# Five homes for x, earlier transposes, and output stores on GpSimd's queue at the end of block 1 of a fused MLP kernel

## The chip, the cores and the metric

The kernel runs on one core of one Trainium2 chip. Times are microseconds (us) on the device, of one execution each; most executions of a kernel agree within 0.3%. A profile shows the span of one execution, from its first to its last instruction. PE is TensorE, DVE is VectorE, ACT is ScalarE, POOL is GpSimd, SP is SyncE; a trailing q (ACTq, SPq) is an engine's queue as it issues a transfer.

## The reference

```
y   = x @ w1 + b1            # x: 16 x 512 x 768, w1: 768 x 3072
y   = 0.5*y*(1 + erf(y/sqrt(2)))
out = y @ w2                 # w2: 3072 x 768, float32 out
```

## The kernel before

The rows are worked in eight blocks of 1024. A block's first product and gelu are units of one kind (`Unit1`), its second product units of others. Both products save multiplications by a Strassen-like scheme: sums of operands on VectorE, seven products instead of eight on TensorE. Block 1 ends in four "lean" units (`Unit2` with `lean`) that finish its second product and store the output, while SP writes prepared weight pieces to memory for later blocks (`w2s`), loads w1 for block 2 (`w1s`), and transposes x of block 2. All SBUF space is cut from one tile, so every home is a range that something else held before.

The parts that the change and the argument touch, with cuts marked:

```python
osbs1 = [[cut(XT_N + k * PAR, 2 * N2).bitcast(FP32),            # right half of an output row tile
          cut(XT_N + k * PAR + 2 * N2, 2 * N).bitcast(FP32)]    # full output row
         for k in range(2)]
spare = stage + [wb_at(2 * XT_N + o) for o in
                 (PAR, PAR + WB, XT_N, XT_N + WB, XT_N + 2 * WB)]
# ...
def xh_of(sb, t):                        # where x of block sb, tile t is loaded
    if sb < ONE:
        return cut(sb * GR + GR // 2 + t * K, K)
    return xh_late[t % 3]                # three homes
# ...
class Unit2:
    def __init__(self, g, sb, u):
        self.lean = sb > 0
        self.eng = nc.scalar if self.lean and u < 2 * NU - 1 else nc.sync   # stores' queue
        self.o = (osbs1 if self.lean else osbs)[u % 2]
    def right_done(self):
        self.eng.dma_start(out=orr[...], in_=self.o[0])         # L471
    def left_done(self, row, bank):
        # ...
        self.eng.dma_start(out=orr[...], in_=self.o[1])         # L482
# ...
def copy_xy(u):                          # seeds PSUM bank bY before products 7, 6, 4
    if isinstance(u, Unit2) and u.lean:
        nc.scalar.copy(out=bY[...], in_=u.rows(par1))           # L618
        return
    nc.scalar.copy(out=bY[...], in_=bX[...])                    # L620
```

## Time and profile before

| | first profiled execution | timed executions |
|---|---|---|
| time | 854.49 us | 851.46, 851.83, 851.99 us |
| span | 852.7 us | |
| PE busy, PE idle | 844.6, 8.1 us | |
| PE waits behind ScalarE, 222 to 236 us | 1.19 + 0.38 + 0.81 us | |

The prediction below shows the lines behind this table. The transfer side of the same stretch, by windows of time (busy us of PE, PEld, DVE, ACT and POOL, then clock, share of the 16 transfer engines, GB/s), before:

```profile
212.00:218.00 6.00, 6.00 (x38) 3.61 (x37) 5.31 (x8) 0.46 (x1) 0.00 (x0) 1.00 1.00 263
218.00:224.00 6.00, 4.82 (x31) 2.83 (x29) 2.69 (x5) 0.89 (x2) 0.53 (x1) 1.00 0.98 141
```

### The profile page before, as it was taken

To read this page: it belongs to the slowest core of one execution; us is meant where nothing else is said; L and a number is where in the kernel's file an instruction comes from. 1 tells how busy PE (TensorE), PEld (TensorE's weight loads), DVE (VectorE), ACT (ScalarE), POOL (GpSimd) and SP (SyncE) were. 2 spreads that over 40 slices of the span, in tenths; PEclk is the share of its full clock that TensorE was granted. 3 is DMA by queue.
4 is the path that set the end of the run, shared out by engine and by line. 5 is a ranking of instruction groups with operands and counts; after the bars stand their busy time and mean duration, and the time that the engine had idled before them with its cause. 6 is when DMAs were issued, how large, how long until landed. Compare 5 with 4: busy or idle time off the path is not lost.

```text
span 852.7 us, 16579 instructions
## 1 busy us (share of the span) xinstructions
PE 844.6 (99%) x6468; PEld 571.2 (67%) x6468; DVE 671.4 (79%) x1132; ACT 422.8 (50%) x692; POOL 85.9 (10%) x139
## 2 busy tenths in 40 slices
PE   9999999999999999999999999999999999999998
PEld 5444445696544798448974499645995469944798
DVE  5766679777756998579976799667996689956998
ACT  4777762221178512784138732577216771267611
POOL 5121100012000002100020000200012100010000
PEclk9999999999999999999999999999999999999999
DMA  9998787579999599996999689995999949985397
GB/s 229 197 282 172 165 187 276 211 217 215 249 353 226 175 318 379 293 203 228 330 367 314 128 279 336 359 276 133 312 346 343 299 106 318 351 323 171 100 306 287
DMA packets 144642, 220.82 MB, mean 259 GB/s; under 512 B 61916, under 2 KB 85396, under 8 KB 144564
## 3 DMA queue, kind: packets, MB, share of 16 engines
q1 hardware_dynamic: 117536, 178.36, 66.7%
q0 software_dynamic: 25696, 38.94, 21.0%
q10 hardware_dynamic: 1332, 2.47, 1.0%
q8 instruction: 50, 0.82, 0.4%
q14 instruction: 28, 0.23, 0.1%
HBM read 182.07 MB, written 47.87 MB: 270 GB/s over the span
## 4 chain that ended last, share of the span: by engine, by line
PE 92%; DMA 6%; DVE 1%; issue 0%; ACT 0%; POOL 0%; ACTq 0%; DVEq 0%
PE bY L409 21%; PE bY L514 15%; PE bX L409 14%; PE bX L514 10%; PE bZ L409 7%; PE bW L409 7%; PE bW L514 5%; PE bZ L514 5%; PE bY L454 3%; DMA arena<-in_x_dram 3%; DMA w2s<-arena 1%; PE bY L601 1%; DMA arena<-in_w_dram 1%; PE bW L454 1%; PE bX L601 1%; PE bZ L454 1%
## 5 line engine op out<-in xcount | busy, mean ns | idle before, releaser
L206 DVE TENSOR_TENSOR arena<-arena 128x1536 f16<-128x1536 f16 (+6 forms) x634 | 406.5, 672 | 7.8 <-DMA arena<-arena 1.3
L409 PEld LDWEIGHTS <-arena 128*128 128x128 f16 x1974 | 192.3, 98 | 226.0 <-issue 2.2
L514 PEld LDWEIGHTS <-arena 128*128 128x128 f16 x3528 | 292.1, 98 | 8.2
L409 PE MATMUL bY<-arena 128*128 128x512 f16 x846 | 214.5, 379 | 1.4 <-ACT bY L620 1.2
L627 DVE TENSOR_TENSOR arena<-bY,arena 128x512 f32<-128x512 f32 (+1 forms) x102 | 69.4, 680 | 121.9 <-PE bY L409 91.9
L620 ACT COPY bY<-bX 128x512 f32<-128x512 f32 (+1 forms) x144 | 79.1, 549 | 123.2 <-DVE arena L563 87.6
L514 PE MATMUL bY<-arena 128*128 128x192 f16 x1500 | 138.3, 246 | 0.0
L409 PE MATMUL bX<-arena 128*128 128x512 f16 x564 | 138.2, 379 | 0.0
L425 ACT ACTIVATE arena<-arena,b1t 128x1024 f16<-128x1024 f32 x94 | 108.0, 1149 | 52.9 <-DVE arena L655 52.9
L640 ACT COPY arena<-bW 128x512 f32<-128x512 f32 (+1 forms) x148 | 81.4, 550 | 89.1 <-PE bW L514 43.9
L514 PE MATMUL bX<-arena 128*128 128x192 f16 x1020 | 93.2, 246 | 0.0
L655 DVE TENSOR_TENSOR arena<-bZ,arena 128x512 f32<-128x512 f32 (+1 forms) x102 | 69.3, 679 | 20.2 <-PE bZ L409 18.2
L409 PE MATMUL bW<-arena 128*128 128x512 f16 x282 | 76.2, 379 | 0.0
L409 PE MATMUL bZ<-arena 128*128 128x512 f16 x282 | 76.2, 379 | 0.0
L546 POOL DMA_DIRECT2D out_dram<-arena x42 | 30.5, 728 | 409.1 <-DVE arena L651 331.8
L430 ACT ACTIVATE arena<-bX,b1t 128x512 f16<-128x512 f32 x94 | 64.0, 680 | 11.1 <-PE bX L409 7.9
L454 PEld LDWEIGHTS <-arena 128*128 128x128 f16 x480 | 46.8, 98 | 32.4 <-issue 1.6
L671 ACT COPY bZ<-bY 128x512 f32<-128x512 f32 (+1 forms) x58 | 30.8, 532 | 70.8 <-DVE arena L655 27.5
L430 ACT ACTIVATE arena<-bY,b1t 128x512 f16<-128x512 f32 x94 | 63.3, 673 | 0.0
L314 POOL DMA_DIRECT2D arena<-in_x_dram x60 | 32.6, 549 | 183.2 <-DMA arena<-arena 172.5
L514 PE MATMUL bZ<-arena 128*128 128x192 f16 x504 | 48.5, 246 | 0.0
L514 PE MATMUL bW<-arena 128*128 128x192 f16 x504 | 48.5, 246 | 0.0
(60 smaller groups left out, 411.1 us busy)
## 6 DMA issues: line engine op xcount, KB each, us to landing
arena<-w2s SPq DMA_DIRECT2D x300, 288.0 KB, 4.6
arena<-w1s SPq DMA_DIRECT2D x72, 672.0 KB, 7.4
out_dram<-arena POOLq DMA_DIRECT2D x42, 384.0 KB, 7.4
w2s<-arena SPq DMA_DIRECT2D x49, 288.0 KB, 4.2
arena<-in_x_dram POOLq DMA_DIRECT2D x60, 192.0 KB, 7.4
w1s<-arena SPq DMA_DIRECT2D x12, 672.0 KB, 6.1
arena<-in_w_dram POOLq DMA_DIRECT2D x17, 384.0 KB, 9.2
out_dram<-arena SPq DMA_DIRECT2D x9, 384.0 KB, 2.5
```

The lines of the kernel that those rows point to most:

```text
L206: nc.vector.tensor_tensor(out=o, in0=a, in1=b, op=op)
L314: nc.gpsimd.dma_start(out=xhs[t], in_=xr[:, sb * 8 + t, :])
L409: nc.tensor.matmul(out=dst[:, 0:RH], lhsT=w1_op(self.wt, slot)[:, c, :], rhs=a[:, c, :], start=first and c == 0, stop=c == self.C - 1, ski ...
L425: nc.scalar.activation(out=self.G[1][:, hi, :, :], in_=self.tmp, func=GELU, bias=b1t[:, 2 * hi + 1:2 * hi + 2])
L430: nc.scalar.activation(out=self.G[0][:, hi, row, :], in_=bank[:, 0:RH], func=GELU, bias=b1t[:, 2 * hi:2 * hi + 1])
L454: nc.tensor.matmul(out=dst[:, 0:N2], lhsT=a, rhs=w[:, :, c, :], start=first and c == 0, stop=c == self.C - 1, skip_group_check=True)
L514: nc.tensor.matmul(out=dst[:, t * N4:(t + 1) * N4], lhsT=a, rhs=w[:, c, :], start=first and c == 0 and t == ts[0], stop=c == NQ - 1, skip_ ...
L620: nc.scalar.copy(out=bY[u.g % 2][:, 0:u.F], in_=bX[u.g % 2][:, 0:u.F])
L627: nc.vector.tensor_tensor(out=u.c22(), in0=bY[u.g % 2][:, 0:u.F], in1=w[:, 0:u.F], op=ADD)
L640: nc.scalar.copy(out=w[:, 0:u.F], in_=bW[:, 0:u.F])
L655: nc.vector.tensor_tensor(out=u.c12(), in0=bZ[:, 0:u.F], in1=w[:, 0:u.F], op=ADD)
L671: nc.scalar.copy(out=bZ[:, 0:u.F], in_=bY[u.g % 2][:, 0:u.F])
```

## The change

Its intent: x of block 2 gets five homes in place of three, so that more of it can be loaded and transposed early; its last transposes are issued a unit sooner (at the end of the first of the four lean units in place of the second); the output stores of the last four units move from ScalarE's queue to GpSimd's; and the full output row gets a third tile. To make room, one of the spare homes of weight pieces goes.

```diff
-    osbs1 = [[cut(XT_N + k * PAR, 2 * N2).bitcast(FP32),
-              cut(XT_N + k * PAR + 2 * N2, 2 * N).bitcast(FP32)] for k in range(2)]
+    osbs1 = [[cut(XT_N + 6 * N + k % 2 * 2 * N2, 2 * N2).bitcast(FP32),
+              cut(XT_N + k % 3 * 2 * N, 2 * N).bitcast(FP32)] for k in range(NU)]
...
-                     (PAR, PAR + WB, XT_N, XT_N + WB, XT_N + 2 * WB)]
+                     (PAR, PAR + WB, XT_N, XT_N + WB)]
+    xh_mid = [cut(2 * XT_N + XT_N + 2 * WB + k * K, K) for k in (2, 3, 4, 0, 1)]
...
-            return xh_late[t % 3]
+            return xh_mid[t % 5 if t < 5 else t - 5] if sb == ONE else xh_late[t % 3]
...
-                self.eng = nc.scalar if self.lean and u < 2 * NU - 1 else nc.sync
-                self.o = (osbs1 if self.lean else osbs)[u % 2]
+                self.eng = nc.gpsimd if self.lean else nc.sync
+                self.o = osbs1[u - NU] if self.lean else osbs[u % 2]
...
-                split_w2(5, (10, 6, 7, 8))
+                split_w2(5, (6, 7, 8, 9))
...
                 if m == 1:
-                    load_next_x(2, range(3))
+                    load_next_x(2, range(5))
                 if m == 3:
                     for t in range(3):
                         transpose_dma(2, t)
-                    load_next_x(2, range(3, 6))
+                    load_next_x(2, range(5, 8))
+                    for t in range(3, 5):
+                        transpose_dma(2, t)
...
             if k == 0 and slot == 6:
-                for t in range(3, 6):
-                    transpose_dma(2, t)
-                load_next_x(2, range(6, 8))
-            if k == 1 and slot == 6:
-                for t in range(6, 8):
+                for t in range(5, 8):
                     transpose_dma(2, t)
```

The new lines shift the numbers: L471, L482, L618 and L620 of before are L473, L484, L620 and L622 of the changed kernel.

More of the change, by code (lines that the diff above doesn't have):

```diff
@@ L186 @@
     spare = stage + [wb_at(2 * XT_N + o) for o in
-                     (PAR, PAR + WB, XT_N, XT_N + WB, XT_N + 2 * WB)]
+                     (PAR, PAR + WB, XT_N, XT_N + WB)]
+    xh_mid = [cut(2 * XT_N + XT_N + 2 * WB + k * K, K) for k in (2, 3, 4, 0, 1)]
+    assert XT_N + 2 * WB + 5 * K == GR // 2
     hyb_w = {2: {7: stage[0], 5: stage[1], 6: stage[2], 4: stage[5]},
```

## The prediction

> **What bounds the kernel now.** I read the busy table first, then the chain that ended last, then TensorE's own waits, then the time lines of TensorE and ScalarE where those waits lie. The page shows
>
> ```profile
> PE 844.6 (99%) x6468; PEld 571.2 (67%) x6468; DVE 671.4 (79%) x1132; ACT 422.8 (50%) x692; POOL 85.9 (10%) x139
> PEclk9999999999999999999999999999999999999999
> PE 92%; DMA 6%; DVE 1%; issue 0%; ACT 0%; POOL 0%; ACTq 0%; DVEq 0%
> ```
>
> The reader is to see that TensorE (PE) is the bound: busy 844.6 of 852.7 us at full clock, and 92% of the last-ending chain. A change that takes away no matmul can return only PE's idle time, 852.7 - 844.6 = 8.1 us (0.95%). So faster by over 2% (17 us) is ruled out by one subtraction. How much of the 8.1 us does this change address? The waits of PE, and its time line at the end of block 1 (start, duration, then in brackets the idle time before it and its releaser):
>
> ```profile
> PE bY L409 <- ACT bY L620: 1.2, 2, 0.8
> PE bY L454 <- ACT bY L618: 1.2, 1, 1.2
> ...
> 223.41 2.11 PE L454 MATMUL bY<-arena 128*128 128x384 f16 x12 [1.19 <-ACT bY L618]
> ...
> 231.17 0.81 PE L409 MATMUL bY<-arena 128*128 128x512 f16 x3 [0.38 <-ACT bY L620]
> ...
> 236.02 1.46 PE L409 MATMUL bY<-arena 128*128 128x512 f16 x6 [0.81 <-ACT bY L620]
> ```
>
> Three gaps, all between 222 and 236 us, all ended by a ScalarE copy into a PSUM bank bY: 1.19 + 0.38 + 0.81 = 2.38 us. The other 5.7 us lie at the start-up, at the tail and in slivers, where the diff has no line. ScalarE itself is hardly busy here, so why were its copies late? Its time line (ACTq is its queue issuing a transfer):
>
> ```profile
> 219.62 0.34 ACTq L471 DMA_DIRECT2D out_dram<-arena  x1
> 222.50 0.34 ACTq L482 DMA_DIRECT2D out_dram<-arena  x1
> 222.88 0.48 ACT L618 COPY bY<-arena 128x384 f32<-128x384 f32 x1 [6.00 <-DMA w2s<-arena]
> ...
> 230.17 0.34 ACTq L482 DMA_DIRECT2D out_dram<-arena  x1
> 230.55 0.57 ACT L620 COPY bY<-bX 128x512 f32<-128x512 f32 x1 [4.52 <-DMA out_dram<-arena]
> ...
> 234.41 0.34 ACTq L482 DMA_DIRECT2D out_dram<-arena  x1
> 234.79 0.69 ACT L430 ACTIVATE arena<-bX,b1t 128x512 f16<-128x512 f32 x1 [3.17 <-DVE arena L627]
> ```
>
> Each late copy stands directly behind an output store on ScalarE's own queue and starts 0.38 us after the store's issue. The first waited 6.00 us for a transfer, w2s<-arena, which has nothing to do with the copy. The compiled order explains it: transfers of the SP and ACT queues take eight completion counters in turn, in program order, and an issue first waits for its counter's previous holder. The store issued at 222.50 shares a counter with a weight put that SP issued at 210.48 and that landed at 222.42 (11.95 us in the chain), in a stretch full of transposes and w1 loads. So SP's backlog stops ScalarE, and ScalarE stops PE.
>
> **What the Trainium skill says.** "PSUM — Partial Sum Buffer", Engine vs sequencer instructions: ScalarE's queue is strict FIFO. The trace agrees: 222.50 issue, 222.88 copy. "Perfetto Trace Analysis", DMA Instruction — HWDGE: the semaphore wait before an issue and the data movement after it are both outside the issue's slice. The trace agrees: the slices are 0.34 us while ScalarE idled 6.00 us. "DMA: Bandwidth & Descriptors", Issuing engines are not separate DMA queues: the work runs on the same 16 engines whoever issues it. So the change buys no transfer time, only an unblocked queue; before, the DMA share is 0.98 to 1.11 in every stretch from 199 to 236 us, so transfers are indeed the crowded resource there. "SBUF — State Buffer", Who interferes with whom: a GpSimd-issued transfer can be starved by VectorE through a shared port. The 42 ordinary GpSimd output stores took 725 to 745 ns each to issue with VectorE 79% busy, so I see no such starvation here.
>
> **The change part by part.**
> (a) Eight output stores leave ScalarE for GpSimd (the compiled order lists all eight on ScalarE's queue before). From ScalarE's path this takes eight issues of 0.34 us, 2.7 us, which cost nothing themselves, and the waits in front of them, which cost PE the 2.38 us. GpSimd gains eight issues at 0.65 to 0.73 us (rows of its existing stores), 5 to 6 us, while it is busy 10% of the span and holds no arithmetic. GpSimd's transfers have counters of their own, so SP's backlog no longer reaches them. ScalarE's L618 will then wait only for VectorE's release of the bank, at about 218.4; PE needs the result at 222.2. The first gap goes with nearly 4 us to spare. L620 at 230.55 needs the bX product, done about 226.1, and the bank released by the VectorE add that ended 227.9; with PE 1.19 us earlier its need is at about 229.6. The second gap goes. The third copy stood behind the issue at 234.41, then an activation of 0.69 us; its bank and product were there before, so it goes too. Gain: 2.38 us.
> (b) The third output row (three full-row tiles, right halves still two) replaces two. VectorE lost 3.3 us at 222.38 waiting for a store to free a row. Now unit 3 reuses unit 0's row some 18 us after its issue; unit 2 reuses unit 0's right half after about 13 us. Median landing of a GpSimd store is 7.4 us, longest 10.1, so both should be free. Off PE's path if so; cost 0.
> (c) Five homes for x: two of the eight x loads, 384 KB read each, move from 194-196 to about 183 us, and the last transposes from 211-227 to about 200-211. No bytes are added. In the old place VectorE waited 1.30 us for a transpose at 226.44 before the x sums. In the new one those waits vanish; both lay beside PE work, so 0 on PE directly, though they ensure that (a) is not handed to a transpose wait.
> (d) The fifth spare home for weight pieces is given up: one series reuses the homes 6, 7, 8, 9 of the series before. The first reuse is VectorE's at about 189.5, its put was issued at 181.2 with a median landing of 4.0 us; the second 193.6 against 183.4. Margins of 4 us or more, even if the two extra x loads add about 768 KB / 214 GB/s = 3.6 us (an estimate from the rate in 172-193 us). Cost 0.
> Matmul and VectorE instruction counts are the same in both compiled programs. Sum: 851.83 - 2.38 = 849.45, so **849.5 us**.
>
> **The rivals.** First, a wait that takes the place of the removed one: a GpSimd store lands late in the saturated stretch, VectorE waits for the output tile, the bank is released late and PE waits again. For it: the DMA share about 1.0, and stores here of up to 9.4 us. Against: 13 us of room. It would return 0.5 to 2 us: 850 to 851.5. Second, GpSimd becomes a new head of line: the stores stand behind x loads that wait for transposes 0 to 2 (released at 194.5 to 196.8 before). If those slip by 10 us, the stores slip, and as above PE pays 1 to 3 us. Against: the first store is ready only at 208.2. Third, the reverse: the gaps were already covered by something else as late, say VectorE's x sums, needed by PE at about 228 and 231. Then only the first gap goes: 850.6. Against: VectorE starts these sums at 226.44 only because a transpose was late. Fourth, more than 2.38 us comes back because the w1 loads of block 2 arrive earlier. Against: PE has no transfer wait in block 2 to recover.
>
> **Range and chances.** Three times of before span 0.53 us, so noise is some 0.3 us each way. All gaps gone gives 849.5, two thirds gone about 850.3, a rival in full 851.5. I choose 848.8 to 851.0. Faster by over 2% would take twice the whole idle time of PE: 0.005. Slower by over 2% needs a new 17 us stall, against waits of at most 12 us in this stretch: 0.01. Within 2%: 0.985.
>
> **What would show each step.** (a) no ACTq issue left in 205-236 us, PE's gaps behind L618 and L620 gone, PE idle down from 8.1 to about 5.7 us with the same busy time. (b) VectorE's 3.3 us wait for out_dram gone. (c) no transposes of block 2 after about 212 us, VectorE's 1.30 us wait gone. (d) no VectorE wait on w2s<-arena around 189-201. Wrong if PE shows a new wait on VectorE or a transfer between 185 and 240 us, or if gaps of the same size turn up later, where the three were only the first place at which a shared lag came to light.

## The result, and the profile after

The changed kernel takes 852.19 us (median of six, 851.51 to 852.39) beside 851.88 us of before (six, 851.46 to 853.48). The ratio, 1.0001 with a 95% interval of 0.9988 to 1.0014, is the mean time of one kernel's fast runs over that of the other's of the same rounds, so not quite the ratio of those medians. There is no gain.

The profile of the changed kernel, however, looks just as forecast. Its busy row and its chain:

```profile
span 850.3 us, 16583 instructions
PE 843.9 (99%) x6468; PEld 571.3 (67%) x6468; DVE 671.1 (79%) x1132; ACT 423.6 (50%) x692; POOL 89.9 (11%) x147
PE 98%; DMA 1%; ACT 0%; DVE 0%; SPq 0%; issue 0%; ACTq 0%
```

All that PE waits for in it lies in the first 10 us:

```profile
PE bX L756 <- DVE arena L742: 1.2, 1, 1.2
PE bT L330 <- DVE arena L762: 1.1, 2, 0.9
```

On PE's time line the three places stand without a gap (222.38, 229.59 and 233.47 are the counterparts of 223.41, 231.17 and 236.02), and ScalarE's copies come when VectorE has freed their bank:

```profile
222.38 2.11 PE L456 MATMUL bY<-arena 128*128 128x384 f16 x12
...
229.59 0.81 PE L411 MATMUL bY<-arena 128*128 128x512 f16 x3
...
233.47 1.46 PE L411 MATMUL bY<-arena 128*128 128x512 f16 x6
```

```profile
218.75 0.48 ACT L620 COPY bY<-arena 128x384 f32<-128x384 f32 x1 [1.56 <-DVE arena L208]
...
225.43 0.57 ACT L622 COPY bY<-bX 128x512 f32<-128x512 f32 x1 [0.43 <-PE bY L456]
```

Profile against profile, the span fell by 2.4 us, the very amount. Time against time, nothing fell. The two can only both hold if the first profile showed an execution that was not like the timed ones, or if the profiler itself made the gaps.

### The profile page after: what moved, and what is told of

It is laid out like the page before. It is cut to its first block, busy times and chain, and to the rows that moved or that the text cites. A ratio compares the mean times of both kernels' runs of the same rounds, so it can differ in the third digit from the quotient of the medians.

```text
span 850.3 us, 16583 instructions
## 1 busy us (share of the span) xinstructions
PE 843.9 (99%) x6468; PEld 571.3 (67%) x6468; DVE 671.1 (79%) x1132; ACT 423.6 (50%) x692; POOL 89.9 (11%) x147
## 4 chain that ended last, share of the span: by engine, by line
PE 98%; DMA 1%; ACT 0%; DVE 0%; SPq 0%; issue 0%; ACTq 0%
PE bY L411 21%; PE bY L516 15%; PE bX L411 14%; PE bX L516 10%; PE bW L411 7%; PE bZ L411 7%; PE bZ L516 5%; PE bW L516 5%; PE bY L456 5%; PE bZ L456 2%; PE bW L456 2%; PE bY L603 1%; PE bX L603 1%; PE bX L456 1%; DMA arena<-in_x_dram 1%; PE bX L778 0%
## 5 line engine op out<-in xcount | busy, mean ns | idle before, releaser
L622 ACT COPY bY<-bX 128x512 f32<-128x512 f32 (+1 forms) x144 | 79.1, 549 | 118.2 <-DVE arena L565 81.5
```

Source lines behind the costliest of these rows:

```text
L622: nc.scalar.copy(out=bY[u.g % 2][:, 0:u.F], in_=bX[u.g % 2][:, 0:u.F])
```

## The experiments

### Are the gaps there in ordinary executions?

The kernel before went to the chip three times more, and the changed one once more. Theory A says that the gaps belong to some executions only, B that they are in all and the change pays them back elsewhere, C that the profiler makes them.

> The kernel before, unchanged, once more. Its first profiled execution took 854.49 us (span 852.7) while its timed runs have a median of 851.88 us, 2.6 us less, which is about the 2.38 us of TensorE gaps I meant to remove. Theory A (the gaps belong to some executions only): this profile shows a span near 850.0 us, TensorE idle near 5.7 us and less than 0.5 us of TensorE waits behind L618 and L620. Theory B (the gaps are in every execution and the change pays them back elsewhere): the gaps of 1.19, 0.38 and 0.81 us are there again at 222-236 us, within 20%. Theory C (the profiler makes them): gaps and a span of 852-853 us here, with the timed runs at 851.9 us.

> The changed kernel, unchanged, once more. Theories A and C: span 850.0 to 850.6 us, no TensorE wait in 205-240 us, timed runs 851.5 to 852.4 us as before, ratio to the kernel before 0.999 to 1.001. Theory B: the same profile, and a loss of about 2.4 us against the kernel before visible somewhere else in it.

> The kernel before a third time, for how often the gaps come. Theory A: no gaps or smaller ones, span 850 to 851.5 us. Theories B and C: 1.19, 0.38, 0.81 us again, span 852-853 us.

> The kernel before a fourth time. Theory A: span 850 to 851.5 us unless this is one of the rare long executions (one of six timed runs took 853.48 us); theories B and C: gaps again, span 852-853 us.

| execution with a profile | time, us | span | unit 1's row store issues (L482) | its copy L618 starts | the matmul behind it starts | PE gap there |
|---|---|---|---|---|---|---|
| before, first profile | 854.49 | 852.7 | 222.50 | 222.88 | 223.41 | 1.19 |
| before_r1 | 851.42 | 849.6 | 220.67 | 221.05 | 221.90 | 0 |
| before_r2 | 851.80 | 850.0 | 219.99 | 220.53 | 222.24 | 0 |
| before_r3 | 852.20 | 850.4 | 221.73 | 222.11 | 222.64 | 0.21 |
| after | 852.12 | 850.3 | on GpSimd, 219.02 | 218.75 | 222.38 | 0 |

after_r1 has a span of 850.7 us and no such gap either. Timed in five rounds, before_r1 has a ratio of 1.0004 [0.9990, 1.0017] to the kernel before (itself) and after_r1 of 1.0003 [0.9990, 1.0015]: the two kernels cannot be told apart. Here are PE's waits in before_r1, and ScalarE's time line there:

```profile
PE bX L754 <- DVE arena L740: 1.2, 1, 1.2
PE bT L328 <- DVE arena L760: 0.3, 1, 0.3
```

```profile
218.95 0.34 ACTq L471 DMA_DIRECT2D out_dram<-arena  x1
220.67 0.34 ACTq L482 DMA_DIRECT2D out_dram<-arena  x1
221.05 0.48 ACT L618 COPY bY<-arena 128x384 f32<-128x384 f32 x1 [4.33 <-DMA w2s<-arena]
```

The reader is to see that the queueing I described is there as well: the copy again stands 0.38 us behind a store that waited for a weight put, 4.33 us this time. But it ends at 221.53, and PE asks for it at 221.90. A wait that ends before it is needed costs nothing, and there were 0.4 us to spare. In before_r3 the room was just used up:

```profile
PE bY L454 <- ACT bY L618: 0.2, 1, 0.2
```

So A holds. B falls, because the gaps are absent or 0.2 us in the three repeats; C falls, because profiled executions without gaps exist (whether profiling makes them more likely, one case in four can't tell). What made the transfers of the first execution so slow is not shown. In 218 to 224 us they moved 141 GB/s there; in the same window of before_r1:

```profile
218.00:224.00 6.00, 6.00 (x39) 3.62 (x37) 4.23 (x7) 0.89 (x2) 1.07 (x3) 1.00 1.15 273
```

The scatter that remains between ordinary executions is at the start, where PE waits for the first tiles of x: those waits on bT came to 0.3, 0.7 and 1.4 us in before_r1, r2 and r3, whose spans are 849.6, 850.0 and 850.4 us. The change does not touch them.

### The parts alone

`stores_only` is the kernel before with one line of the change; `act_stores` is the changed kernel with that line undone.

```diff
-    self.eng = nc.scalar if self.lean and u < 2 * NU - 1 else nc.sync
+    self.eng = nc.gpsimd if self.lean else nc.sync
```

> The kernel before with the eight stores on GpSimd's queue and nothing else, no extra copies. With the copies it took 5 us longer, because VectorE waited 4.7 us for a transpose. If the late transposes are a danger by themselves: a VectorE wait for a transpose of over 2.5 us and TensorE idle 0.3 to 2 us behind it, time 852.3 to 854. If it took the copies to make them late: no TensorE wait, time within 0.3 us of the kernel before.

> The changed kernel with the eight stores back on ScalarE's queue, no extra copies. If the early transposes take the backlog away: ScalarE's store of unit 1 issues before 220.5 us, no TensorE wait, time within 0.3 us of both kernels. If ScalarE's stores are the danger whatever the transposes do: store at 221 us or later, TensorE waits 0.2 to 2 us, 852.3 to 854 us.

stores_only took 852.35 us (ratio 1.0010 [0.9997, 1.0022]), act_stores 851.52 us (0.9997 [0.9984, 1.0011]); neither has a PE wait in 205 to 240 us. Neither beats the kernel before. The forecast for stores_only was met in its waits and missed in its time: 0.60 us over the kernel before, not within 0.3, though the interval of the ratio includes 1. For act_stores it was met beside the kernel before (0.23 us under it) and missed beside the changed one, which took 852.19 and 852.11 us in other rounds. What differs is the room. In act_stores, with the transposes out of the way, unit 1's store leaves ScalarE's queue without having to wait for SP's backlog:

```profile
218.44 0.34 ACTq L484 DMA_DIRECT2D out_dram<-arena  x1
218.82 0.48 ACT L620 COPY bY<-arena 128x384 f32<-128x384 f32 x1 [1.94 <-DVE arena L208]
```

PE's matmul behind that copy starts at 222.06, so the copy, done at 219.30, has 2.8 us to spare, against none to 1.2 in the kernel before. In stores_only the copy is as early (218.59). Each part alone restores the room at this place, and the second adds nothing to it in an ordinary execution.

### The same parts with more transfers

If the change has a worth, it shows when transfers are late. So two copies of 672 KB within DRAM, which take no part in the result, were added on GpSimd's queue near 210 us:

```diff
+    junk = [dp.tile([P, 7 * KQ * P], F16, name=f"junk{n}") for n in range(2)]
...
+            if k == 1 and slot == 5:
+                for n in range(2):
+                    nc.gpsimd.dma_start(out=junk[n][:], in_=w1s[5][:])
```

> The kernel before with two extra DRAM-to-DRAM copies of 672 KB each, issued by GpSimd at about 210-212 us, which take no part in the result and load the transfers just where the weight put stands that ScalarE's store waits for. Two copies of 672 KB are about 5 us of transfers at the 260 GB/s seen there. Theory A (the mechanism is right, but an ordinary execution has 0.1 to 1.6 us of room left): the store at 220-221.7 us slips to 223-226, TensorE waits 1 to 4 us behind L618, time 1 to 4 us over the kernel before. Theory D (there is no lever here: the room is larger than it looks, or TensorE waits for w1 instead): TensorE waits on transfers or on nothing, not behind ScalarE's copies.

> The changed kernel with the same two extra copies. Theory A: no TensorE wait behind L620 and L622, time within 0.5 us of the changed kernel, so 1 to 4 us under the kernel before with the copies. Theory D: as much longer as the kernel before with the copies. My first rival (late GpSimd stores hold up VectorE): a VectorE wait for out_dram and a TensorE wait of 0.5 to 2 us.

> The kernel before with the eight stores on GpSimd's queue and nothing else of the change, and the two extra copies. If the queue alone is what protects TensorE: no wait behind ScalarE's copies, time as for the changed kernel with the copies. If the third row or the earlier transposes are needed too: VectorE waits 2 to 6 us for out_dram at unit 2 (3.3 us in the first profile) or for a transpose before the x sums, and TensorE 0.5 to 3 us.

> The changed kernel with the eight stores back on ScalarE's queue, and the two extra copies: five homes, early transposes and third row stay. If the queue alone protects: TensorE waits 0.5 to 4 us behind the copies. If the earlier transposes, by emptying SP's backlog after 212 us, protect as well: less than 0.5 us of such waits.

In act_stores_s2 the copies went out at 203.9 us, among the transposes, because nothing stood ahead of them on GpSimd's queue. It took 851.72 to 868.82 us, two of its four runs slow, so its time does not compare. Its profile, of a slow run of 865.67 us, missed both forecasts: PE stood 11.62 us behind ScalarE's copy, against 0.5 to 4 us or under 0.5 us. It was made again with the copies behind a one-element GpSimd copy that reads unit 0's finished row, which holds them until 211.2 us:

```diff
+                nc.gpsimd.tensor_copy(out=gate[:], in_=osbs1[0][1][:, 0:1])
```

> As act_stores with the two extra copies, but these wait for unit 0's row (about 211 us), as in the changed kernel with the copies. In act_stores_s2 they went out at 203.9 us, among the transposes, which may be why it lost 10 us. If the timing of the copies was the cause: under 2 us over the kernel before, TensorE wait behind L621 under 2 us. If ScalarE's queue was: 5 to 15 us again.

| with the two copies | copies issued | stores on | transposes | ratio to before without copies | PE gap in 205 to 240 us, behind |
|---|---|---|---|---|---|
| before_s2 | 209.0 | ScalarE | late | 1.0016 [1.0001, 1.0031] | 1.55, ScalarE's copy L619 |
| stores_only_s2 | 211.5 | GpSimd | late | 1.0063 [1.0046, 1.0081] | 2.60, VectorE's x sum |
| act_stores_s3 | 211.2 | ScalarE | early | 1.0019 [1.0002, 1.0036] | 0.82, ScalarE's copy L624 |
| after_s2 | 211.5 | GpSimd | early | 1.0007 [0.9991, 1.0024] | none |

Each row is the profile of one execution; the ratio rests on four. In act_stores_s3 one of the four took 856.23 us, which no profile caught. PE and ScalarE in before_s2, where the first profile's gap is made to order:

```profile
223.48 2.11 PE L455 MATMUL bY<-arena 128*128 128x384 f16 x12 [1.55 <-ACT bY L619]
```

```profile
222.43 0.47 ACTq L483 DMA_DIRECT2D out_dram<-arena  x1
222.95 0.48 ACT L619 COPY bY<-arena 128x384 f32<-128x384 f32 x1 [6.37 <-DVE arena L656]
```

The bracket names a VectorE sum that ends at 222.53 us, after the store has gone out at 222.43, so the store waited for something else: the weight put that SP issued at 211.56 landed 10.80 us later, at 222.36. In act_stores_s3 the tie shows again, at unit 2. PE, then ScalarE, whose store follows a put that landed at 229.09:

```profile
230.17 0.81 PE L413 MATMUL bY<-arena 128*128 128x512 f16 x3 [0.82 <-ACT bY L624]
```

```profile
229.17 0.34 ACTq L486 DMA_DIRECT2D out_dram<-arena  x1
229.55 0.57 ACT L624 COPY bY<-bX 128x512 f32<-128x512 f32 x1 [4.96 <-DMA out_dram<-arena]
```

In stores_only_s2 ScalarE is on time and PE still stops, because the last transpose has not landed for VectorE's x sum. PE, then VectorE:

```profile
229.48 1.44 PE L410 MATMUL bW<-arena 128*128 128x512 f16 x3 [2.60 <-DVE arena L207]
```

```profile
228.46 0.96 DVE L207 TENSOR_TENSOR arena<-arena 128x1536 f16<-128x1536 f16 x1 [4.69 <-DMA arena<-arena]
```

This kernel lost 5.05 us beside the kernel before (857.07 against 852.02 us), more than its gap. The granted clock fell as well; here are the two windows from 224 to 236 us (columns as above):

```profile
224.00:230.00 6.00, 3.40 (x19) 1.71 (x17) 1.54 (x3) 0.48 (x2) 0.00 (x0) 0.95 1.14 251
230.00:236.00 6.00, 6.00 (x26) 2.75 (x25) 4.67 (x7) 1.93 (x4) 1.08 (x2) 0.76 1.04 399
```

An estimate from these clocks, 6 x 0.05 + 6 x 0.24, puts that at 1.7 us.

The copies went out 2.5 us sooner in before_s2 than in stores_only_s2, so these two differ in more than the queue. The last three rows share the moment, 211.2 to 211.5 us, and among them each half of the change, the queue or the rest, leaves one way of being late open, and only both together leave PE without a gap. What the third output row does by itself was not tested. With copies before_s2 comes to 853.40 us and after_s2 to 852.70 us. The difference of 0.70 us is under half of the 1.55 us gap and the intervals overlap: a gain in time is not shown. The expectation of 1 to 4 us for the kernel before was met at its lower end (1.38 us); that of 1 to 4 us between the two kernels was missed. My first rival, late GpSimd stores, did not come true here: after_s2 has no VectorE wait for out_dram.

### Where the protection ends

The copies were also put among the transposes of the changed kernel, on GpSimd's queue ahead of its stores (`k == 0 and slot == 6` in place of `k == 1 and slot == 5`).

> The changed kernel with the two extra copies at about 204 us, among the transposes, as in act_stores_s2. If the timing of the copies was the cause there: transposes take until 213 us here too and w1 for block 2 comes at 226 us or later, so TensorE waits 2 to 10 us, now for transposes or w1 rather than for ScalarE. If ScalarE's queue was: no TensorE wait behind ScalarE, time under 1 us over the changed kernel.

> after_s4 again, for a profile of a long execution. If GpSimd's queue removes the danger at its root: a long execution shows TensorE waiting for w1 or for a transpose, not behind ScalarE or VectorE. If it only moves the head of the line: VectorE waits several us for out_dram or a transpose, ScalarE's copy follows, and TensorE waits 5 to 10 us behind one of the two.

> The same, a second chance to catch a long execution; three of four were 861 to 863 us.

Four timed executions took 853.18, 863.02, 861.34 and 863.38 us (ratio 1.0100 [1.0057, 1.0142]); the profile fell on the first. The two further looks caught long ones, 863.02 and 864.61 us. PE's wait in after_s4b, and its windows (columns as above):

```profile
232.99 1.46 PE L412 MATMUL bX<-arena 128*128 128x512 f16 x3 [8.94 <-DMA arena<-w1s]
```

```profile
212.00:218.00 6.00, 6.00 (x39) 3.62 (x37) 5.43 (x8) 0.46 (x1) 0.54 (x1) 1.00 1.07 94
218.00:224.00 6.00, 6.00 (x38) 3.42 (x35) 2.37 (x4) 0.89 (x2) 0.54 (x1) 1.00 1.04 103
230.00:236.00 6.00, 3.01 (x9) 1.35 (x10) 3.83 (x5) 0.57 (x1) 0.54 (x1) 0.50 0.88 286
```

SP's queue, the changed kernel and then after_s4b, shows part of why w1 is late: the same three transposes hold it for 6 us in one and for 15 us in the other, and w1 stands behind them.

```profile
201.06 6.01 SPq L322 DMA_TRANSPOSE arena<-arena  x3
...
207.79 3.43 SPq L236 DMA_DIRECT2D arena<-w1s  x2
```

```profile
201.08 15.09 SPq L323 DMA_TRANSPOSE arena<-arena  x3
216.26 1.30 SPq L274 DMA_DIRECT2D w2s<-arena  x1
217.66 13.80 SPq L237 DMA_DIRECT2D arena<-w1s  x2
```

The other part is the load's own landing. The chain that ended last, in after_s4b and then in act_stores_s2:

```profile
217.66 15.28 DMA arena<-w1s
```

```profile
215.40 17.42 DMA arena<-w1s
```

The same load took 4.69 us in the changed kernel; at that pace it would have landed by about 222.4 us in after_s4b, before PE stopped at 224.05 (an estimate). Why transposes and loads were so slow is not shown: in the fast execution of the same kernel, after_s4, the transposes held SP's queue for 8.12 us and 323 and 355 GB/s were moved in the windows from 212 to 224 us.

No ScalarE copy is involved any more; PE waits for the weights themselves (9.18 us in after_s4c). In act_stores_s2 the same load stopped ScalarE's store and through it PE, for 11.62 us; with the stores on GpSimd it stops PE directly, for 8.94 us. VectorE waits 6.8 us for out_dram besides, which is my first rival, but PE's long wait outlasts it. So ScalarE's queue was only one of the ways by which a late transfer reaches PE.

## Why the prediction was wrong

The bound and the ceiling were right: PE is busy 99%, and nothing over 2% could come. The mechanism was right as well: unit 1's store left ScalarE's queue 0.08 us after SP's weight put had landed, at 222.42, 220.59, 219.91 and 221.65 us in the four profiles of the kernel before. Step (a): no transfer issue is left on ScalarE's queue between 205 and 240 us, the gaps are gone, and PE's idle time in the profile is 850.3 - 843.9 = 6.4 us; the 0.7 us over the forecast 5.7 is the start-up wait on bT, 1.1 us in place of 0.4. GpSimd's busy time grew by 4.0 us, less than the forecast 5 to 6. Step (b): VectorE's 3.3 us wait for out_dram is gone. Step (c): the last three transposes are issued from 201.06 to 207.07, and VectorE's 1.30 us wait is gone. Step (d): no VectorE wait on w2s appears, and the instruction counts on PE and VectorE are the same. But what (b) and (c) took away was not in the repeats of the kernel before either: VectorE has no out_dram wait in any of the three, and a transpose wait of 0.8 us in one. One reading was loose: only the first two copies start 0.38 us after a store; the third, at 235.38, stands 0.97 us behind it with an activation between.

**The step that failed** is the term "1.19 + 0.38 + 0.81 us = 2.38 us" and its use in "851.83 - 2.38 = 849.45". The gaps were read in an execution of 854.49 us and taken off the median of others. In the three repeats the term measures 0, 0 and 0.21 us. Put in its place, the sum gives some 851.8 us, within the scatter of what was measured. The other 2.4 us were never in the median: 854.49 less 2.38 is 852.11, which is what the changed kernel's profiled execution took, 852.12. That this fits to 0.01 us is luck: between the two profiles PE's idle time fell by 1.7 us and its busy time by 0.7.

The sentence on noise, "three times of before span 0.53 us", failed with it: the fourth known time lay 2.5 us above the highest of those three. The range was built on the three.

Of the rivals, the one that came nearest is the third, gaps that are covered anyway, but for a reason that I did not name: they are covered by room on ScalarE's side, not by an equally late VectorE. The first came true, for VectorE only, in after_s4b and after_s4c (6.8 and 6.5 us). The second and the fourth did not show: in the changed kernel GpSimd issued its first store at 208.84 us. The last clause of the prediction, that the gaps might be only where a shared lag came to light, fits after_s4b, with its added copies, where the lag came to light at w1.

What stays open: why the transfers of the first execution were slow from 218 to 224 us, how often such executions come, and why the kernel of after_s4 takes 853 us in one execution and 861 to 865 us in others. One of four profiles of the kernel before has a large gap there and one a gap of 0.2 us. Among its 39 other executions without extra copies three are above 853 us, among eleven of the changed kernel none; that is too few to claim a narrower spread.

## What to carry to other kernels

Before taking a gap off the median, set the time of the profiled execution beside the timed ones; if it is longer by about the size of the gap, take a second profile first. A late copy costs only what is left after its room, so measure the room (when it ended, when it was needed) in several executions. And a change that clears one queue guards against late transfers only along that queue: to see what it is worth, make the transfers late on purpose, with each part alone.

## What the Trainium skill lacked or had wrong

- "DMA: Bandwidth & Descriptors" gives a bandwidth, constraints and a correctness rule for transposes; it says nothing of what they cost next to bulk copies. Here three transposes held SP's queue for 6.01 us, and with two 672 KB copies in flight for 8.12 us in one execution and 15.09 us in another; in the latter the whole core moved 94 to 103 GB/s in the 12 us after 212 us with its transfer engines fully busy.
- "TensorE: Matmul & The Clock Gate", Part 1, puts the fall to half clock after an idle window of about 3.4 us. The half rate agrees (clock 0.50 in 230 to 236 us of after_s4b, after 8.94 us idle), but in stores_only_s2 a wait of 2.60 us was enough: the clock averaged 0.76 in the 6 us that followed 230 us, and single microseconds there show 0.50. A wait of 1.19 us left it at 1.00.
- No page has it that completion counters dealt out in turn tie two queues together: a ScalarE store waited for an SP put in flight 11.95 us, and ScalarE sat idle for 6.00 us.
- No page says to check, by its time, that the profiled execution is like the timed ones: 854.49 against 851.83 us here was the whole of the forecast gain.
